# Weight gradient by Strassen pairs: sums carried by accumulating transfers, copies over two banks, and a twenty-fourth pair

## The chip, the core and the metric

The kernel runs on one core of a Trainium2 chip. The metric is the device time of one execution in microseconds, as the median of several runs. A profile of one execution goes with it; its span counts from the first to the last instruction on the core and is a little shorter than the metric (161.5 us against 163.29 us for the same run).

## The reference

```python
def setup_inputs():
    batch, m, k, n = 16, 512, 1024, 768
    input       : (batch, m, k) float32, random normal
    grad_output : (batch, m, n) float32, random normal

def reference(input, grad_output):
    return np.einsum('bmk,bmn->kn', input, grad_output).astype(np.float32)
```

So 8192 rows (16 x 512) of `input` and `grad_output` are contracted: out = X^T G, 1024 x 768. The rows are cut into 64 slabs of 128, and the result into four quarters: A and B are the upper 512 rows (k), C and D the lower ones; A and C take one half of the 768 columns (384), B and D the other. Each quarter has four banks' worth of result: q = 0 to 3, each 128 x 384.

## The kernel before

**Loads.** The slabs come in by twos. A unit u is two slabs (256 rows), and the transfers issued by GpSimd round float32 to bfloat16 on the way. `LOADS` says what a unit is: `s`, two slabs taken singly, or `P`, a pair.

```python
LOADS = "sssssssPPPPPPPPPPPPPPPPPPPPPPPss"      # 9 s, 23 P
PAIRS_HELD = 14                                  # buffers for units
...
for u, kind in enumerate(LOADS):
    ...
    if u >= MERGED:
        nc.gpsimd.dma_start(out=gp, in_=G[rows, :].rearrange("(p m) n -> p m n", m=2))
        nc.gpsimd.dma_start(out=xp, in_=X[rows, :].rearrange("(p m) k -> p m k", m=2))
    ...
    # an s unit becomes two items, a P unit one item
```

**Products.** A single slab costs 16 matmuls of 128 x 384: four quarters by four banks. A pair of slabs is handled as a 2 x 2 block product with seven products instead of eight (Strassen): `m n o p q`, kept in `macc`, and two that go straight to quarters A and D. That is 28 matmuls in place of 32, for five sums of operands on VectorE.

```python
def sum_g1(i): ... nc.vector.tensor_add(ge (128x1152), g[0:3*NH], g[NH:4*NH])
def sum_g2(i): ... nc.vector.tensor_sub(g[0::3], g[0::3], g[2:0:-1])
def sum_x1(i): ... nc.vector.tensor_add(xe[0:2], xp[0], xp[1])
def sum_x2(i): ... nc.vector.tensor_add(xe[2], ...)
def sum_x3(i): ... nc.vector.tensor_sub(x[1:3], x[1:3], x[0::3])
```

At the end the five products are shared out: A gets m + p - q, B gets o + q, C gets n + p, D gets m + o - n. In the kernel before VectorE does this with the operations named in `SHARES`, except that -q goes to A as the first contents of A's banks (the step `A38:0-q`).

```python
SHARE_OF = {
    "t1": ("m", "o", 0), "t2": ("p", "q", 0), "t3": ("q", None, 0),     # to A and B
    "l1": ("n", "m", Q), "l2": ("p", "o", Q), "l3": (None, "n", Q),     # to C and D
}
SHARES = ("l20 l21 l22 t20 t21 t22 t10 t11 t12 t13 l23 t23 l10 l11 l12 l13 l30 l31 l32 l33 ").split()
...
op(out=dst, in0=dst, in1=src)     # 128 x 768 where both sides are served, else 128 x 384
```

**Steps.** PSUM has eight banks, two groups of four. `ORDER` lists the steps: which sum (A to D, m to q) takes its items up to which number next, how many of its four banks ScalarE handles (after `:`), whether the sum is closed, that is emptied to SBUF, at the end of the step (`!`), and how many operations of the filler (operand sums, then shares) VectorE does ahead of each bank. A bank that ScalarE handles is first filled with the sum so far (`carry`), and the matmuls add to it; a bank that VectorE handles is added to the sum after the matmuls.

```python
ORDER = (
    "A1:3!0,0,0,0 C1:1 B1:3 B2!0,0,0,0 C2!0,0,0,0 D2:3 A2 D3 A3 D4!0,0,0,0 A4 B4:1^!0,0,0,0 C4 "
    "C6!0,0,0,0 A6!0,0,0,0 D6:2~!0,0,0,0 B6:3^ C8!0,0,0,0 ... "
    # ... cut ...
    "q23!3,0,0,0 m21:4~ m23!2,1,0,0 n21:4~ A38:0-q n23!5,0,0,1 A40 B18:4!2,1,0,1 A41!0,0,0,0 "
    "C17:3 C18!1,0,0,0 D41!3,0,0,0 "
).split()

def carry(m, slot, q):                                     # before the matmuls
    if q >= Q - byact:
        bank = psum.tile([P, 512], f32, name=f"bank{slot * Q + q}")[:, 0:NH]
        nc.scalar.copy(out=bank, in_=sum_of(p, q))         # L296
...
def mm(q, j):
    nc.tensor.matmul(bank, stat, mov, ...)                 # L337
...
def shut(q):                                               # after them
    fill(ahead[q])
    if act:        nc.scalar.copy(out=dst, in_=bank)               # L353
    elif fresh[p]: nc.vector.tensor_copy(out=dst, in_=bank)        # L355
    else:          nc.vector.tensor_add(out=dst, in0=bank, in1=dst)  # L357
    if final and p in "ABCD":
        nc.sync.dma_start(out=OUT[...], in_=dst)           # L360, the quarter's rows leave
```

The last bank of the last step is made in two pieces (L392, added at L400), so that its store starts sooner. At the start, twelve matmuls on constants (L96) warm TensorE, and the first two slabs are loaded as float32 and rounded by VectorE and ScalarE (L211).

```python
round_by("DVE", x0, xf[0], 0, P)            # columns of the first slab, in this order
round_by("ACT", x0, xf[0], 2 * P, 4 * P)
round_by("DVE", x0, xf[0], P, 2 * P)
round_by("DVE", x0, xf[0], 4 * P, 6 * P)
round_by("ACT", x0, xf[0], 6 * P, 8 * P)
...
if n == 1: round_by("DVE", g0, gf, 0, NH)   # right half of the first slab's gradient
```

Of the kernel before, what the change touches and what calls it, by code (L numbers as in the profile page):

```python
# [8 lines left out]

P = 128  # L10

LOADS = "sssssssPPPPPPPPPPPPPPPPPPPPPPPss"

ORDER = (
    "A1:3!0,0,0,0 C1:1 B1:3 B2!0,0,0,0 C2!0,0,0,0 D2:3 A2 D3 A3 D4!0,0,0,0 A4 B4:1^!0,0,0,0 C4 "
    "C6!0,0,0,0 A6!0,0,0,0 D6:2~!0,0,0,0 B6:3^ C8!0,0,0,0 B8!0,0,0,0 D8:2~!0,0,0,0 A8!0,0,0,0 "  # L20
    "D9:2 B10!0,0,0,0 D10!0,0,0,0 A10 B12:2^!0,0,0,0 A12!0,0,0,0 D12:3 B14!0,0,0,0 D14!0,0,0,0 "
    "C13:3^ C14!6,0,0,0 A15:1 1o2:4!1,1,1,0 q2:4!0,1,0,1 A16!0,0,0,0 D16:1^ p3:4!2,1,1,0 "
    "D17!0,0,0,0 n3:2 1o4:3!2,0,0,1 n4!0,0,0,0 m4:4!1,1,1,2 p5:1^!0,0,0,0 A19:3^!0,0,0,1 q4:4~ "
    "2q6!2,0,1,0 D20!1,0,0,0 o7:4~!0,1,1,1 n7:2^!1,0,0,1 m7:1^!1,0,0,0 p8:1~ 2A22:4!2,1,0,2 "
    "p9!0,0,0,0 D23:3~!0,0,1,0 q9:3^ 2q10!2,0,0,0 o10:2^!1,0,0,0 n10:2^ 2n11!2,0,0,0 "
    "A25:4~!1,0,1,0 m10:2^ 2m12!2,0,0,0 D26!1,0,0,0 p13:4~!0,1,2,1 o13:3~!0,0,1,1 q12:3~ "
    "2A28:2~!2,0,0,1 q13!0,0,0,0 n15:3~!2,0,1,1 D28:1^!0,0,1,0 o16:2^!0,0,0,0 q16:2~!2,0,0,1 "
    "m15:3~ 1p17:3^!4,0,1,1 D30!1,0,0,0 m16 m18!0,0,0,0 q18:4~!1,1,0,1 A32 1n19:4^!4,0,1,2 "
    "o20:1~!0,1,0,0 D34:3^ 4D35!1,0,0,0 A35!1,0,0,0 o22:2^ p21:4 5p23!1,0,1,1 o23!0,0,0,0 q21:2~ "
    "q23!3,0,0,0 m21:4~ m23!2,1,0,0 n21:4~ A38:0-q n23!5,0,0,1 A40 B18:4!2,1,0,1 A41!0,0,0,0 "  # L30
    "C17:3 C18!1,0,0,0 D41!3,0,0,0 "
).split()


SHARES = (
    "l20 l21 l22 t20 t21 t22 t10 t11 t12 t13 l23 t23 l10 l11 l12 l13 l30 l31 l32 l33 "
).split()

WARMUP = [512] * 10 + [128] * 2
PAIRS_HELD = 14  # L40
# [6 lines left out]
def kernel(  # L47
# [6 lines left out]
    nc = tc.nc  # L54
    bf16 = mybir.dt.bfloat16
    f32 = mybir.dt.float32

    B, M, K = input.shape
    _, _, N = grad_output.shape
    S = B * M // P  # L60
    KH = K // 2
    NH = N // 2
    Q = KH // P


    LEFT, RIGHT = slice(NH, N), slice(0, NH)
# [24 lines left out]
    nc.scalar.dma_start(out=xf[1], in_=X[P : 2 * P, :])  # L91

    ones = nc.const_aps.tensor(1.0, (P, P), bf16)
    wps = psum.tile([P, 512], f32, name="bank7")
    for cols in WARMUP:
        nc.tensor.matmul(  # L96
            wps[:, 0:cols],
# [105 lines left out]
    def fill(n):  # L203
        for _ in range(n):
            f, i = filler.pop()
            f(i)
# [36 lines left out]
            "A": lambda: (x[:, 1, k], ge[:, 2, :]),  # L243
        }[p]()

    def sum_of(p, q):
        if p in SLOT:
            return macc[:, SLOT[p], q, :]
        row = q if p in "AB" else Q + q
        return acc[:, row, 0:NH] if p in "AC" else acc[:, row, NH:N]  # L250

    done = {p: 0 for p in streams}
    fresh = {p: True for p in streams}
# [4 lines left out]

    def parsed(step):
        step, _, ahead = step.partition("!")  # L260
        step, _, byact = step.partition(":")
        early = byact[-1:] if byact[-1:] in ("^", "~") else ""
        byact = byact.rstrip("^~")
        at = next(c for c in step if c.isalpha())
        before, upto = step.split(at)
        ahead = [int(a) for a in ahead.split(",")] if ahead else None
        return int(before or 0), at, int(upto), int(byact[:1] or 0), byact[1:], early, ahead

    steps = [parsed(step) for step in ORDER]

# [1 line left out]
    def follower(n, free):  # L272
        now = {p for p in opened if p != steps[n][1]}
        shut_since = {steps[n][1]}
        for m in range(n + 1, len(steps)):
            _, p, _, byact, first, early, ahead = steps[m]
            if p not in now:
                if not free:
                    if not early:
                        return None  # L280
                    assert byact and not first and not fresh[p] and p not in shut_since
                    return m
                free -= 1
            now.add(p)
            if ahead is not None:
                now.remove(p)
                shut_since.add(p)
        return None
# [1 line left out]
    filled = {}  # L290

    def carry(m, slot, q):
        p, byact = steps[m][1], steps[m][3]
        if q >= Q - byact:
            bank = psum.tile([P, 512], f32, name=f"bank{slot * Q + q}")[:, 0:NH]
            nc.scalar.copy(out=bank, in_=sum_of(p, q))  # L296
            filled[m, q] = bank

    def visit(n):
        _, p, upto, byact, first, early, ahead = steps[n]  # L300
        close, last = ahead is not None, n == len(steps) - 1
        items_now = streams[p][done[p] : upto]
        done[p] = upto
# [1 line left out]
        if opening:  # L305
            slot = slots.pop(0)
            banks = []
            for q in range(Q):
                name = f"bank{slot * Q + q}"
                act = q >= Q - byact  # L310
                carried = act and not fresh[p]
                if carried:
                    assert name in used
                    if not early:
                        carry(n, slot, q)
                    bank = filled.pop((n, q))
                else:
                    bank = psum.tile([P, 512], f32, name=name)[:, 0:NH]
                if first:
                    assert name in used and not fresh[p] and not byact  # L320
                    src = macc[:, SLOT[first[1]], q, :]
                    if first[0] == "-":
                        nc.scalar.mul(out=bank, in_=src, mul=-1.0)
                    else:
                        nc.scalar.copy(out=bank, in_=src)
                used.add(name)
                banks.append((bank, carried or bool(first), act))
            if first:
                taken.add((p, first[1]))
            opened[p] = (slot, banks)  # L330
# [3 lines left out]
        def mm(q, j):  # L334
# [8 lines left out]
                skip_group_check=carried,  # L343
            )

        follows = follower(n, len(slots)) if close and not last else None

        def shut(q):
            fill(ahead[q])
            bank, _, act = banks[q]  # L350
            dst = sum_of(p, q)
            if act:
                nc.scalar.copy(out=dst, in_=bank)  # L353
            elif fresh[p]:
                nc.vector.tensor_copy(out=dst, in_=bank)  # L355
            else:
                nc.vector.tensor_add(out=dst, in0=bank, in1=dst)  # L357
            if final and p in "ABCD":
                row = q if p in "AB" else Q + q
                nc.sync.dma_start(out=OUT[:, row, LEFT if p in "AC" else RIGHT], in_=dst)  # L360
            if follows is not None:
                for b in ([q] if steps[follows][5] == "^" else range(Q) if q == Q - 1 else []):
                    carry(follows, slot, b)

        if len(items_now) == 1:
            for q in range(Q):
                mm(q, 0)
            if close:
                for q in range(Q):
                    shut(q)  # L370
        else:
            for q in range(Q):
                if last and q == Q - 1 and opening:
                    assert not banks[q][1]
                    break
                for j in range(len(items_now)):
                    mm(q, j)
                if close:
                    shut(q)
            else:  # L380
                q = None
            if q is not None:

                fill(ahead[q])
                dst = sum_of(p, q)
                row = q if p in "AB" else Q + q
                b0 = (LEFT if p in "AC" else RIGHT).start
                for c0, c1, name in ((0, 256, None), (256, NH, f"bank{slots[0] * Q}")):
                    bank = banks[q][0] if name is None else psum.tile([P, 512], f32, name=name)
                    for j in range(len(items_now)):  # L390
                        stat, mov = operands(p, items_now[j], q)
                        nc.tensor.matmul(  # L392
                            bank[:, 0 : c1 - c0],
                            stat,
                            mov[:, c0:c1],
                            start=j == 0,
                            stop=j == len(items_now) - 1,
                        )
                    d = dst[:, c0:c1]
                    nc.vector.tensor_add(out=d, in0=bank[:, 0 : c1 - c0], in1=d)  # L400
                    store = nc.sync if name is None else nc.scalar
                    store.dma_start(out=OUT[:, row, b0 + c0 : b0 + c1], in_=d)
        if close:
            fresh[p] = False
            del opened[p]
            slots.append(slot)

    rounded = False
    for n, (before, p, upto, *_) in enumerate(steps):
# [42 lines left out]
```

## Time and profile before

| what | value |
|---|---|
| time, median of 3 runs | 163.32 us (163.26 to 163.52) |
| span of the profiled execution | 161.5 us |
| TensorE (PE) busy | 157.4 us, 97%, 950 matmuls |
| VectorE (DVE) busy | 140.9 us, 87% |
| ScalarE (ACT) busy | 118.0 us, 73% |
| GpSimd (POOL) busy | 34.8 us, 22%, nearly all of it issuing loads |
| transfers on GpSimd's queue | 28.64 MB, 89.6% of the sixteen DMA engines over the span |
| granted TensorE clock | full throughout |

A matmul's bar in the trace is some 326 ns long, but the next one starts before it ends, so bars overlap; what counts is the step from start to start, which the chain of waits gives. Busy times of the other engines can be compared with the span directly. The DMA share is near full until about 141 us, when the last load has landed, and low after that, except for the stores at the end.

### The profile page before, as it was taken

What the parts mean: (1) busy time and instruction counts of PE and PEld (TensorE: products, weight loads), DVE (VectorE), ACT (ScalarE), POOL (GpSimd) and SP (SyncE); (2) the same over time, 40 slices, a digit from 0 to 9 for tenths busy, and PEclk for the clock granted to TensorE, in tenths of its full rate; (3) what the DMA queues carried; (4) which work ended last, traced back from release to release, by engine and by line L of the source; (5) the groups of instructions that cost most, each with busy time, mean ns of one, the idle gap of its engine ahead of it and who ended that gap; (6) DMA issues with size and microseconds to landing.
All of it is one profiled execution on the core that took longest, in us unless ns stands there. A gap on an engine that the chain in (4) does not pass through costs nothing.

```text
span 161.5 us, 2781 instructions
## 1 busy us (share of the span) xinstructions
PE 157.4 (97%) x950; PEld 92.8 (57%) x950; DVE 140.9 (87%) x267; ACT 118.0 (73%) x278; POOL 34.8 (22%) x69
## 2 busy tenths in 40 slices
PE   8999999999999999999999999999999999999991
PEld 2465655566555565655666665566665656656661
DVE  0545888979889999999999999999998999999982
ACT  3745358446598899978999897997795666987730
POOL 7442222122222212222212222222122100000000
PEclk9999999999999999999999999999999999999999
DMA  5999999999999999999999999999999999900695
GB/s 168 300 213 213 212 214 213 213 215 212 214 212 212 212 211 215 214 214 211 211 214 218 214 213 211 214 212 215 213 211 216 210 214 212 199 11 0 232 354 195
DMA packets 12398, 33.40 MB, mean 207 GB/s; under 512 B 1376, under 2 KB 4192, under 8 KB 12384
## 3 DMA queue, kind: packets, MB, share of 16 engines
q0 software_dynamic: 9360, 28.64, 89.6%
q1 hardware_dynamic: 2592, 3.47, 6.1%
q10 hardware_dynamic: 432, 1.11, 1.9%
q8 instruction: 7, 0.11, 0.3%
q14 instruction: 7, 0.06, 0.1%
HBM read 58.72 MB, written 3.15 MB: 383 GB/s over the span
## 4 chain that ended last, share of the span: by engine, by line
PE 84%; DMA 12%; issue 1%; DVE 0%; POOLq 0%
PE bank L337 84%; DMA xp<-in_input_dram 9%; DMA gp<-in_grad_output_dram 4%; PE bank L392 0%; DVE acc L400 0%; POOLq L436 0%
## 5 line engine op out<-in xcount | busy, mean ns | idle before, releaser
L337 PEld LDWEIGHTS <-xp 128*128 128x128 bf16 x650 | 63.3, 98 | 43.5 <-issue 0.8
L337 PE MATMUL bank<-gp,xp 128*128 128x384 bf16 x468 | 81.1, 327 | 0.1
L353 ACT COPY macc<-bank 128x384 f32<-128x384 f32 x91 | 39.4, 493 | 9.7 <-PE bank L337 9.4
L357 DVE TENSOR_TENSOR acc<-bank,acc 128x384 f32<-128x384 f32 x80 | 39.8, 552 | 5.8 <-PE bank L337 5.5
L337 PEld LDWEIGHTS <-xe 128*128 128x128 bf16 x276 | 26.9, 98 | 17.9 <-DVE xe L148 0.2
L353 ACT COPY acc<-bank 128x384 f32<-128x384 f32 x57 | 24.8, 485 | 13.9 <-PE bank L337 13.9
L296 ACT COPY bank<-macc 128x384 f32<-128x384 f32 x73 | 33.0, 496 | 1.6 <-DVE acc L357 0.9
L337 PE MATMUL bank<-ge,xp 128*128 128x384 bf16 x182 | 33.6, 326 | 0.0
L337 PE MATMUL bank<-gp,xe 128*128 128x384 bf16 x184 | 32.4, 326 | 0.0
L296 ACT COPY bank<-acc 128x384 f32<-128x384 f32 x47 | 21.6, 494 | 8.9 <-DVE acc L357 7.2
L114 POOL DMA_DIRECT2D xp<-in_input_dram x30 | 16.0, 532 | 53.0 <-DMA xp<-in_input_dram 30.2
L113 POOL DMA_DIRECT2D gp<-in_grad_output_dram x30 | 16.0, 533 | 37.3 <-PE bank L337 15.0
L357 DVE TENSOR_TENSOR macc<-bank,macc 128x384 f32<-128x384 f32 x35 | 18.1, 553 | 1.3 <-PE bank L337 1.3
L138 DVE TENSOR_TENSOR ge<-gp 128x1152 bf16<-128x1152 bf16 x23 | 17.3, 753 | 0.3 <-DMA gp<-in_grad_output_dram 0.3
L148 DVE TENSOR_TENSOR xe<-xp 128x1024 bf16<-128x1024 bf16 x23 | 15.8, 686 | 1.4 <-DMA xp<-in_input_dram 1.3
L194 DVE TENSOR_TENSOR acc<-acc,macc 128x768 f32<-128x768 f32 (+1 forms) x20 | 16.1, 875 | 0.0
L337 PE MATMUL bank<-ge,xe 128*128 128x384 bf16 x92 | 15.9, 326 | 0.0
L157 DVE TENSOR_TENSOR xp<-xp 128x1024 bf16<-128x1024 bf16 x23 | 15.8, 687 | 0.0
L143 DVE TENSOR_TENSOR gp<-gp 128x768 bf16<-128x768 bf16 x23 | 12.8, 555 | 0.5
L152 DVE TENSOR_TENSOR xe<-xp 128x512 bf16<-128x512 bf16 x23 | 9.7, 420 | 0.0
L355 DVE COPY acc<-bank 128x384 f32<-128x384 f32 x6 | 3.2, 555 | 3.3 <-PE bank L337 3.2
L96 PE MATMUL bank<-const-bfloat16-1.0 128*128 128x512 bf16 (+1 forms) x12 | 4.6, 574 | 0.8 <-PEq L436 0.8
(18 smaller groups left out, 15.7 us busy)
## 6 DMA issues: line engine op xcount, KB each, us to landing
xp<-in_input_dram POOLq DMA_DIRECT2D x30, 512.0 KB, 16.7
gp<-in_grad_output_dram POOLq DMA_DIRECT2D x30, 384.0 KB, 16.7
out_dram<-acc SPq DMA_DIRECT2D x15, 192.0 KB, 2.4
xf<-in_input_dram ACTq DMA_DIRECT2D x2, 512.0 KB, 5.0
gp<-in_grad_output_dram POOLq DMA_DIRECT2D x3, 192.0 KB, 6.5
xp<-in_input_dram POOLq DMA_DIRECT2D x2, 256.0 KB, 7.8
gf<-in_grad_output_dram SPq DMA_DIRECT2D x2, 192.0 KB, 4.3
out_dram<-acc SPq DMA_DIRECT2D x1, 128.0 KB, 1.9
```

Of the source, the lines that this page charges most:

```text
L113: nc.gpsimd.dma_start(out=gp, in_=G[rows, :].rearrange("(p m) n -> p m n", m=2))
L114: nc.gpsimd.dma_start(out=xp, in_=X[rows, :].rearrange("(p m) k -> p m k", m=2))
L138: nc.vector.tensor_add(out=ge.rearrange("p a n -> p (a n)"), in0=g[:, 0 : 3 * NH], in1=g[:, NH : 4 * NH])
L143: nc.vector.tensor_sub(out=g[:, 0::3, :], in0=g[:, 0::3, :], in1=g[:, 2:0:-1, :])
L148: nc.vector.tensor_add(out=xe[:, 0:2, :].rearrange("p a k -> p (a k)"), in0=xp[:, 0, :], in1=xp[:, 1, :])
L152: nc.vector.tensor_add(out=extra[i][0][:, 2, :], in0=xp[:, 0, 0:KH], in1=xp[:, 1, KH:K])
L157: nc.vector.tensor_sub(out=x[:, 1:3, :], in0=x[:, 1:3, :], in1=x[:, 0::3, :])
L194: op(out=dst, in0=dst, in1=src)
L296: nc.scalar.copy(out=bank, in_=sum_of(p, q))
L337: nc.tensor.matmul(bank, stat, mov, start=opening and j == 0 and not carried, stop=close and j == len(items_now) - 1, skip_group_check=car ...
L353: nc.scalar.copy(out=dst, in_=bank)
L357: nc.vector.tensor_add(out=dst, in0=bank, in1=dst)
```

## The change

The change has three named parts, and a new list of steps that goes with them.

- **A twenty-fourth pair.** The seventh unit of `LOADS` becomes a pair; eight `s` units and 24 `P` units remain.
- **Copies over two banks.** PSUM becomes one tile `ps` of eight banks, and a step may say (`@` and four bits) that two neighbouring banks are emptied, or filled, by one instruction of 128 x 2 x 384 instead of two.
- **Accumulating transfers.** When the last part of m, p or o has reached `macc`, a transfer issued by GpSimd adds the complete product to a quarter: m to D, p to C, o to D, each 128 x 4 x 384 float32. Product n goes to C as the first contents of C's banks (`C16:0+n`). VectorE keeps t1, t2, t3 and l3, and l1 and l2 are gone.

Their purpose is fewer matmuls, fewer instructions on ScalarE and VectorE, and fewer shares for VectorE near the end.

```diff
-LOADS = "sssssssPPPPPPPPPPPPPPPPPPPPPPPss"
+LOADS = "ssssssPPPPPPPPPPPPPPPPPPPPPPPPss"
 ORDER = (
-    "A1:3!0,0,0,0 C1:1 B1:3 B2!0,0,0,0 C2!0,0,0,0 D2:3 A2 D3 A3 D4!0,0,0,0 A4 B4:1^!0,0,0,0 C4 "
-    "C6!0,0,0,0 A6!0,0,0,0 D6:2~!0,0,0,0 B6:3^ C8!0,0,0,0 B8!0,0,0,0 D8:2~!0,0,0,0 A8!0,0,0,0 "
-    ... cut ...
+    "C1:3@1!0,0,0,0 B1:3@9 A2:1@7!0,0,0,0 B2@f D3:1@7 B3@9!0,0,0,0 D4@2!0,0,0,0 A4:1^@4!0,0,0,0 "
+    "C4@2!0,0,0,0 B4:2^@9 B6@9!0,0,0,0 D6:2~@e!0,0,0,0 C6@4 D8:2@8!0,0,0,0 C8@5!0,0,0,0 B8:1^@2 "
+    "A8:1^@5 ... "
+    ... cut ...
+    "q23:4@8 4q24@d!0,2,0,0 p24@6!0,0,0,0 n24@f!0,2,0,0 m24:4@f!0,0,0,0 B14 o24:3^@3!3,1,0,1 "
+    "B16!3,0,0,0 A40@9!0,2,0,0 C16:0+n@6!0,0,0,0 D40@3!4,0,0,0 "
 ).split()
 SHARES = (
-    "l20 l21 l22 t20 t21 t22 t10 t11 t12 t13 l23 t23 l10 l11 l12 l13 l30 l31 l32 l33 "
+    "t20 t21 t22 t23 t30 t31 t10 t11 t12 t13 t32 t33 l30 l31 l32 l33 "
 ).split()
+ADDED = "mD pC oD".split()
...
+    ps = psum.tile([P, 2 * Q, 512], f32, name="ps")
...
 def carry(m, slot, q):
         if q >= Q - byact:
-            bank = psum.tile([P, 512], f32, name=f"bank{slot * Q + q}")[:, 0:NH]
-            nc.scalar.copy(out=bank, in_=sum_of(p, q))
+            both = wide[2 + q // 2] and (q - q % 2) >= Q - byact
+            if both and q % 2 == 0:
+                return
+            b = q - both
+            nc.scalar.copy(out=ps[:, slot * Q + b : slot * Q + q + 1, 0:NH], in_=sum_of(p, b, q + 1))
...
 def shut(q):
+            both = wide[q // 2] and act == banks[q ^ 1][2] and not pieces
+            if both and q % 2 == 0:
+                return
             fill(ahead[q])
-            bank, _, act = banks[q]
-            dst = sum_of(p, q)
+            b = q - both
+            bank = ps[:, slot * Q + b : slot * Q + q + 1, 0:NH]
+            dst = sum_of(p, b, q + 1)
...
+        if final and p in SLOT:
+            for quarter in (pair[1] for pair in ADDED if pair[0] == p):
+                ...
+                nc.gpsimd.dma_start(
+                    out=sum_of(quarter, 0, Q), in_=sum_of(p, 0, Q), accum_op=mybir.AluOpType.add
+                )
```

The order in which the first slab's columns are rounded is not changed.

## The prediction

> **What bounds the kernel now.** I read the chain of waits first, because with 97% on TensorE the question is what sets its start and what follows its end.
>
> ```profile
> 1.23 6.26 DMA gp<-in_grad_output_dram
> 7.50 0.28 issue
> 7.78 13.91 DMA xp<-in_input_dram
> 21.68 0.04 issue
> 21.73 135.51 PE bank L337 x830
> 157.25 0.67 PE bank L392 x6
> ...
> 157.94 0.63 DVE acc L400 x2
> ```
>
> The columns are start, length and what. From 21.73 us to the end the chain is TensorE and nothing else: 830 matmuls in 135.51 us, 163.3 ns from start to start. Before that it is a load. All 128x384 matmuls at L337 are 932 - 6 = 926, so 926 - 830 = 96 were done at 21.73 us. The list of steps agrees: ahead of C8, the first step that uses items 6 and 7 (the fourth unit, u=3), stand six slabs of 16 matmuls. So TensorE stood there for u=3's `xp`. The waits of the weight loads, which stand for TensorE's, and the trace in order of time say how long:
>
> ```profile
> PEld L337 <- issue: 0.8, 4, 0.2
> PEld L337 <- DMA xp<-in_input_dram: 0.7, 2, 0.5
> PEld L337 <- DVE xp L211: 0.3, 1, 0.3
> PEld L337 <- DVE xe L148: 0.2, 1, 0.2
> ```
>
> ```profile
> 16.21 5.03 PEld L337 LDWEIGHTS <-xp 128*128 128x128 bf16 x32 [0.19 <-DMA xp<-in_input_dram]
> ...
> 21.73 4.34 PEld L337 LDWEIGHTS <-xp 128*128 128x128 bf16 x28 [0.48 <-DMA xp<-in_input_dram]
> ```
>
> Two waits for data, 0.19 and 0.48 us; after the second, nothing stops TensorE for more than 0.2 us. Next, the other engines and the transfers by stage (TensorE, weight loads, VectorE, ScalarE, GpSimd busy; clock, DMA share, GB/s):
>
> ```profile
> 100.00:120.00 20.00, 20.00 (x125) 12.05 (x124) 19.86 (x40) 17.87 (x43) 5.07 (x10) 1.00 1.07 213
> ...
> 140.00:145.00 5.00, 5.00 (x32) 2.95 (x31) 5.00 (x7) 4.91 (x13) 0.00 (x0) 1.00 0.26 52
> 145.00:150.00 5.00, 5.00 (x33) 3.03 (x31) 5.00 (x7) 3.80 (x10) 0.00 (x0) 1.00 0.00 0
> 150.00:155.00 5.00, 5.00 (x33) 2.96 (x31) 4.88 (x10) 3.39 (x9) 0.00 (x0) 1.00 0.84 301
> ```
>
> VectorE and ScalarE are nearly full, yet TensorE never waits for them: time saved on them buys nothing by itself. Loads end near 141.3 us (0.26 of the stage from 140 us).
>
> **What the Trainium skill says.** "TensorE: Matmul & The Clock Gate" (Wait — 56ns, not 53.3ns?) gives N / 2.4 GHz + 2.5 ns for back-to-back matmuls, 162.5 ns for N = 384; the trace's 163.3 agrees, so only the count of matmuls and waits can move the stretch. "ScalarE: Activation LUTs" (What ACT_TABLE_LOAD costs) has 0.833 ns per element on top of a fixed cost; the trace's 485 to 496 ns for 384 elements fit, and I use it for the copy over two banks. "DMA: Bandwidth & Descriptors" (SWDGE vs HWDGE vs iDMA) says that accumulation is for GpSimd's queue alone and that this has one context: such a transfer stands behind all loads issued earlier. The loads' 16.7 us from issue to landing show how long that queue is. The page gives no rate for accumulation and no trace here has one.
>
> **The change, part by part.** The rows for the copies and sums (busy us, mean ns):
>
> ```profile
> L357 DVE TENSOR_TENSOR acc<-bank,acc 128x384 f32<-128x384 f32 x80 | 39.8, 552 | 5.8 <-PE bank L337 5.5
> ...
> L357 DVE TENSOR_TENSOR macc<-bank,macc 128x384 f32<-128x384 f32 x35 | 18.1, 553 | 1.3 <-PE bank L337 1.3
> ...
> L194 DVE TENSOR_TENSOR acc<-acc,macc 128x768 f32<-128x768 f32 x16 | 14.1, 955 | 0.0
> ```
>
> *Matmuls.* Singles 16 slabs x 16 = 256, pairs 24 x 28 = 672: 928 against 18 x 16 + 23 x 28 = 932. Four fewer: 4 x 163.3 ns = **-0.65 us**, on the path.
>
> *Start.* In the new list item 6 is first used by D8. Ahead of it stand 88 matmuls, not 96: six slabs less A's share of items 4 and 5, which now comes in A8, after D8. u=3's load has nothing changed ahead of it and should land at 21.7 us again. Can TensorE have done 88 by then? The new list opens with C, whose columns are rounded last, and then needs the gradient's right half, which VectorE rounds only after C's first copy. From the starts in the trace (VectorE's three roundings end near 5.4 us, the second slab is rounded from 7.1 us) I get some 11 matmuls done at 8.0 us where the kernel before had 14. 11 + 77 x 0.163 us more is 20.6 us. So yes; it then waits 1.1 us instead of 0.48. Eight matmuls more stand after the wait: 8 x 163.3 ns = **+1.3 us**. From there 834 run up to the last bank, for 830: net **+0.65 us**. Later units come every 4.3 us (next 25.9, 30.2, 34.5 us) and are first used 1 to 2.5 us after landing, at 163.3 ns a matmul counted from 21.7 us, so this is the one data wait that I expect to set the path.
>
> *ScalarE.* By the new list 87 + 65 copies of one bank and 24 + 23 of two, for 148 + 120 of one. Before, 118.8 us for 268, 0.443 each; after, 152 x 0.443 + 47 x (0.443 + 0.32) = 103 us. -16 us, beside TensorE.
>
> *VectorE.* Adds: 57.9 us for 115, 0.503 each; after 72 x 0.503 + 20 x (0.503 + 0.403, from 955 - 552 ns) = 54.3. First copies +1.8. One more pair of sums, (17.3 + 12.8 + 15.8 + 9.7 + 15.8) / 23 = +3.1. Shares: 16.1 before; now 8 wide (t1, t2) at 0.88 and 8 narrow (t3, l3) at 0.503, 11.1. Sum -3.6 + 1.8 + 3.1 - 5.0 = -3.7 us, beside TensorE.
>
> *Transfers.* Each is 128 x 4 x 384 x 4 B = 0.786 MB. By t(n) = 21.7 + (n - 88) x 0.1633 us: p is complete at matmul 796, 137.3 us; m at 820, 141.3; o at 844, 145.2. The last step's first bank is done at matmul 901, 154.5 us. The transfer of p stands behind the last loads, so it starts near 141.3; m's behind it; o's adds to the same bytes as m's and must wait for m's landing. With A us for each, o's lands near 141.3 + 3A + 1.9 (1.9 from the store of 128 KB, as the cost of one landing and a new issue). Then VectorE still has four l3 (2.0), three adds (1.5) and the two pieces (0.63): 4.1 us. Without waiting, VectorE would end at 158.57 + 0.65 = 159.2. **Delay = 3A - 11.9 us**, if positive. For A I take estimates from this trace: 0.786 MB at 301 GB/s (the stores' stage) is 2.6 us; at the loads' 213 GB/s 3.7; at half the stores' rate, since source and destination are both read, 5.2. The first two delay nothing, the last 3.7 us.
>
> **Sum.** 163.32 + 0.65 = 164.0, plus a tail of 0 to 4 us. Weighed, 164.3.
>
> **The rivals.** *One:* the start is as good as before and the four matmuls count in full, 162.7 us. For it: a list this elaborate was plainly fitted, and the other waits vanish. Against it: 88 against 96 is a count, and u=3's landing belongs to the queue. *Two:* the accumulations become the bound, 166 to 170 us. For it: three in a row on one queue, behind the loads, two on the same bytes, and the DMA engines read twice. Against it: the engines are idle from 141.3 to 150 us. *Three:* bank turnover. A two-bank copy frees its first bank later (by 0.32 to 0.4 us), and TensorE waits, 0.5 to 1.5 us in all: 164.5 to 165.5. For it: short steps of four matmuls, 0.65 us. Against it: ScalarE has 16 us more room. *Four:* the lighter engines pay by 2%; nothing supports it, since TensorE waited for neither.
>
> **Range and chances.** No tail, some 55%: 163.6 to 164.5. Bank waits or a tail up to 2.6 us, 20%. A above 4.8 us, over 2% slower, 22%. Rival one and better, little. So 163.3 to 168.0; faster by over 2% 0.01, within 0.77, slower 0.22.
>
> **What would show it.** Right: a wait of about 1 us for `xp` near 20.6 us; 834 matmuls of 163 ns from 21.7 us to the last bank; no accumulation landing after 155 us. Wrong start: u=3's data used later than matmul 88, or landing earlier. Wrong tail: VectorE's l3 released by a transfer after 155 us, and TensorE's end well ahead of VectorE's. Wrong bank argument: weight loads released by ScalarE or VectorE for over 0.5 us in all.

## The result, and the profile after

169.81 us (median of 4 runs, 168.74 to 170.16) against 163.34 us: a ratio of 1.0383, interval 1.0336 to 1.043. The prediction was 164.3 us, in a range of 163.3 to 168.0. The time went where 3A - 11.9 looked for it, into the accumulating transfers at the end, but their cost was larger than reckoned and the way to the first of them was another.

The chain of waits of the kernel after (start, length, what):

```profile
7.67 13.99 DMA xp<-in_input_dram
...
21.71 119.31 PE ps L350 x728
...
142.41 0.74 ACT macc L373
143.15 0.29 issue
143.44 7.84 DMA acc<-macc
...
151.89 8.78 DMA acc<-macc
...
160.69 0.62 DVE acc L199 x2
...
164.05 0.53 DVE acc L421 x2
```

In the kernel before, the chain stayed on TensorE up to VectorE's last pieces. Here it leaves TensorE at 141 us (TensorE itself works on to 159.2 us), passes over ScalarE's last copies of m, and two accumulating transfers take over, m's into D (143.44 us) and o's into D (151.89 us). They are followed by VectorE's l3 shares, last adds and pieces. The start is as it was: TensorE released at 21.7 us by the fourth unit's `xp`. The trace in order of time shows the wait there (in brackets):

```profile
21.70 14.25 PEld L350 LDWEIGHTS <-xp 128*128 128x128 bf16 x89 [1.38 <-DMA xp<-in_input_dram]
21.71 14.47 PE L350 MATMUL ps<-gp,xp 128*128 128x384 bf16 x88 [0.99 <-DMA xp<-in_input_dram]
```

0.48 us before, 0.99 to 1.38 us now. At the other end, the stages show TensorE still at work and VectorE waiting (busy: TensorE, weight loads, VectorE, ScalarE, GpSimd; clock, DMA share, GB/s):

```profile
154.00:155.00 1.00, 1.00 (x9) 0.61 (x7) 0.73 (x1) 0.00 (x0) 0.00 (x0) 1.00 1.02 184
155.00:156.00 1.00, 1.00 (x8) 0.61 (x7) 0.00 (x0) 0.00 (x0) 0.00 (x0) 1.00 1.10 237
...
159.00:160.00 1.00, 0.23 (x5) 0.05 (x1) 0.00 (x0) 0.00 (x0) 0.00 (x0) 1.00 1.14 255
160.00:161.00 1.00, 0.00 (x0) 0.00 (x0) 0.31 (x1) 0.00 (x0) 0.00 (x0) 1.00 1.03 353
```

The DMA engines, which in the kernel before moved nothing from 142 to 150 us and only stores after that, are now full from 142 us on (1.12 from 142 to 150 us), but for about a microsecond around o's issue. TensorE ends at 159.2 us; VectorE starts again at 160.7. The granted clock has no part in this: its mean over the span is 0.987, but it is 1.00 up to 162 us and lower only after TensorE's last matmul. The groups, for the copies over two banks and for VectorE's wait (busy, mean ns, then idle time before them):

```profile
L373 ACT COPY macc<-ps 128x768 f32<-128x768 f32 x17 | 13.6, 801 | 7.9 <-PE ps L350 7.7
...
L377 DVE TENSOR_TENSOR acc<-ps,acc 128x768 f32<-128x768 f32 x8 | 7.6, 952 | 3.9 <-PE ps L350 3.9
...
L199 DVE TENSOR_TENSOR acc<-acc,macc 128x384 f32<-128x384 f32 x8 | 4.1, 550 | 6.0 <-DMA acc<-macc 6.0
```

ScalarE is busy for 104.7 us (118.0 before) and VectorE for 137.3 (140.9): VectorE is relieved by what was reckoned, ScalarE by somewhat less. The issues of the three transfers on GpSimd, in order p, m, o:

```profile
139.31 1.32 POOL L433 DMA_DIRECT2D acc<-macc  x1 [13.24 <-DVE acc L199]
143.44 1.30 POOL L433 DMA_DIRECT2D acc<-macc  x1 [2.80 <-ACT macc L373]
151.89 1.27 POOL L433 DMA_DIRECT2D acc<-macc  x1 [7.16 <-DMA acc<-macc]
```

The third waits 7.16 us for the second's landing, as both write D. What the engines did meanwhile I counted from the DMA packets that the trace lists; each transfer is 512 rows of 1536 B:

| rows of | first row starts, us | last row starts, us | took, us | rows a us |
|---|---|---|---|---|
| p into C | 141.2 | 145.7 | 4.5 | 113 |
| m into D | 145.7 | 150.8 | 5.0 | 102 |
| o into D | 154.1 | 160.1 | 6.0 | 85 |

An accumulated row occupies a DMA engine for 148 ns on average, a stored row of the same size for 70. Between m's last row and o's first lie 3.35 us. p's first row came 1.9 us after p's issue, while rows of the last loads still ran (the last of them started at 141.7 us); m's first came 2.3 us after m's issue and right behind p's last, o's 2.2 us after o's issue.

### The profile page after: what moved, and what is told of

Read it like the earlier page. It is cut to its first block, busy times and chain, and to the rows that moved or that the text cites. A ratio compares the mean times of both kernels' runs of the same rounds, so it can differ in the third digit from the quotient of the medians.

```text
span 167.9 us, 2669 instructions
## 1 busy us (share of the span) xinstructions
PE 157.4 (94%) x949; PEld 92.7 (55%) x949; DVE 137.3 (82%) x248; ACT 104.7 (62%) x209; POOL 38.8 (23%) x72
## 4 chain that ended last, share of the span: by engine, by line
PE 71%; DMA 22%; issue 2%; DVE 1%; ACT 1%; DVEq 0%; POOLq 0%; ACTq 0%
PE ps L350 71%; DMA acc<-macc 10%; DMA xp<-in_input_dram 8%; DMA gp<-in_grad_output_dram 4%; ACT macc L373 1%; DVE acc L199 1%; DVEq L476 0%; DVE acc L377 0%; DVE acc L421 0%; ACT ps L308 0%; POOLq L433 0%; POOLq L476 0%; ACTq L373 0%; POOLq L465 0%
## 5 line engine op out<-in xcount | busy, mean ns | idle before, releaser
L350 PE MATMUL ps<-gp,xp 128*128 128x384 bf16 x444 | 78.0, 327 | 1.1 <-DMA xp<-in_input_dram 1.0
L373 ACT COPY macc<-ps 128x384 f32<-128x384 f32 (+1 forms) x65 | 33.9, 573 | 16.5 <-PE ps L350 16.2
L377 DVE TENSOR_TENSOR acc<-ps,acc 128x384 f32<-128x384 f32 (+1 forms) x54 | 30.6, 608 | 8.0 <-PE ps L350 7.6
L350 PE MATMUL ps<-ge,xp 128*128 128x384 bf16 x187 | 34.8, 326 | 0.0
L350 PE MATMUL ps<-gp,xe 128*128 128x384 bf16 x192 | 33.4, 326 | 0.0
L373 ACT COPY acc<-ps 128x384 f32<-128x384 f32 (+1 forms) x46 | 22.5, 534 | 15.6 <-PE ps L350 15.3
L308 ACT COPY ps<-macc 128x384 f32<-128x384 f32 (+1 forms) x54 | 28.6, 562 | 3.0 <-DVE acc L377 1.4
L377 DVE TENSOR_TENSOR macc<-ps,macc 128x384 f32<-128x384 f32 (+1 forms) x38 | 24.3, 675 | 3.4 <-PE ps L350 3.2
L308 ACT COPY ps<-acc 128x384 f32<-128x384 f32 (+1 forms) x34 | 19.1, 598 | 5.5 <-DVE acc L377 5.3
L350 PE MATMUL ps<-ge,xe 128*128 128x384 bf16 x96 | 17.1, 326 | 0.0
L199 DVE TENSOR_TENSOR acc<-acc,macc 128x768 f32<-128x768 f32 (+1 forms) x16 | 11.1, 749 | 6.0 <-DMA acc<-macc 6.0
L148 DVE TENSOR_TENSOR gp<-gp 128x768 bf16<-128x768 bf16 x24 | 13.3, 554 | 0.6
```

The costliest lines, as they stand in the source:

```text
L148: nc.vector.tensor_sub(out=g[:, 0::3, :], in0=g[:, 0::3, :], in1=g[:, 2:0:-1, :])
L308: nc.scalar.copy(out=ps[:, slot * Q + b : slot * Q + q + 1, 0:NH], in_=sum_of(p, b, q + 1))
L350: nc.tensor.matmul(bank, stat, mov, start=opening and j == 0 and not carried, stop=close and j == len(items_now) - 1, skip_group_check=car ...
```

## The experiments

**o's addition back on VectorE.** (Each diff is against the kernel after, unless it says otherwise.)

```diff
-ADDED = "mD pC oD".split()
+ADDED = "mD pC".split()
-    "... t32 t33 l30 l31 l32 l33 "                      # SHARES
+    "... t32 t33 l20 l21 l22 l23 l30 l31 l32 l33 "
-    "... D40@3!4,0,0,0 "                                # ORDER
+    "... D40@3!8,0,0,0 "
```

> Only o's addition to D goes back from a transfer to VectorE (four additions of 128x384); m to D and p to C stay transfers. Theory 1, the second accumulation on D's bytes sets the end: VectorE waits for m's landing (151.3 us) at most, its stop from 154.7 to 160.7 us disappears, and it runs eight shares, three sums and two pieces from 154.7 us, 8 x 0.49 + 1.5 + 0.6 = 6.0, to some 160.8 us instead of 164.6: about 166.0 us. Theory 2, VectorE's own backlog at the end sets it and the transfer only hides it: 2 us more work, 169.8 to 172 us.

Measured: 165.28 us, ratio 1.012 (1.0081 to 1.016). VectorE in order of time:

```profile
153.90 3.82 DVE L199 TENSOR_TENSOR acc<-acc,macc 128x384 f32<-128x384 f32 x8
157.65 1.47 DVE L377 TENSOR_TENSOR acc<-ps,acc 128x384 f32<-128x384 f32 x3
```

The stop is gone, although VectorE does 2 us more: theory 1. VectorE has no pause left here and ends at 159.65 us, TensorE at 158.5, so part of theory 2 is true of this version: its backlog is the next bound. (In this trace the fourth unit landed 1 us sooner than in that of the kernel after, as the last section tells; the stop is gone by far more than that.)

**Copying instead of adding.** The additions are left out.

```diff
-    out=sum_of(quarter, 0, Q), in_=sum_of(p, 0, Q), accum_op=mybir.AluOpType.add
+    out=sum_of(quarter, 0, Q), in_=sum_of(p, 0, Q)
```

> The three transfers copy the product over the quarter instead of adding to it (the additions are left out). Same queue, same bytes, same waits. Theory 1a, the accumulation as such is slow (147 ns a row of 1536 B on a DMA engine where a stored row takes 67): rows near 70 ns, each transfer's rows done in some 2.2 us instead of 4.3, o's landing near 153 us, no wait of VectorE, 164 to 165 us. Theory 3, it is the place in the queue, the issue and the landing of any such transfer: rows may be faster but o still lands after 158 us, over 167.5 us.

Measured: 164.58 us, ratio 1.0072 (1.0055 to 1.0088). The chain, and the issue of o's transfer:

```profile
21.92 136.03 PE ps L350 x831
157.95 1.50 PE ps L413 x18
...
159.48 0.29 DVE acc L421
```

```profile
148.40 0.75 POOL L433 DMA_DIRECT2D acc<-macc  x1 [3.99 <-DMA acc<-macc]
```

TensorE sets the end again. The queue, bytes and waits are the same, but a transfer now lands 4.4 us after its issue (7.8 when adding), o's at 152.8 us, GpSimd is done with an issue in 0.75 us (1.3 when adding), and the packets hold up to three rows, 191 ns a packet on average and 66 ns a row. So it is the accumulation that is slow, not the place in the queue; theory 3 falls. This run also gives the kernel's time without its tail, 164.6 us.

**Without C's stores.** The four transfers that store quarter C are left out.

```diff
-            if final and p in "ABCD":
+            if final and p in "ABD":
```

> Quarter C is not stored (its four transfers to memory are left out), so that o's accumulation has the DMA engines to itself. Theory 1b, C's stores slow it (85 rows a us where m's had 124): 512 rows in 4.1 us instead of 6.2, 2 us less, about 167.8 us. If the stores only fill gaps: 169.8 us.

Measured: 169.4 us, ratio 1.0357 (1.0316 to 1.0399), which overlaps the interval of the kernel after; the time tells nothing. The packets do: o's rows took 5.35 us instead of 6.0, and its landing came 8.08 us after the issue instead of 8.78. From the chain:

```profile
150.94 8.08 DMA acc<-macc
```

C's stores cost some 0.7 us, not 2. The expected 2 us rested on 124 rows a us for m; the count gives 102 in the kernel after, which would have made it 1 us. What the other quarters' stores cost was not tried.

**A's items 4 and 5 ahead of C6.**

```diff
-D6:2~@e!0,0,0,0 C6@4
+D6:2~@e!0,0,0,0 A6!0,0,0,0 C6@4
```

> A takes items 4 and 5 in a step of its own ahead of C6, so that 96 matmuls and not 88 stand before the first use of the fourth unit. TensorE's wait of about 1 us goes, its end comes 1.3 us sooner (near 157.9 us). Theory 1, the tail is the transfers': p's rows wait for the loads and m's for p's, all as before, so 169.8 us, less than 0.5 us of change. Theory 4, the start and TensorE still count: 168.5 us.

Measured: 169.03 us, ratio 1.0345 (1.033 to 1.0361). TensorE's wait for the fourth unit is gone, its longest wait for a load 0.2 us. The issues of the three transfers, and VectorE's last pieces:

```profile
138.35 1.32 POOL L433 DMA_DIRECT2D acc<-macc  x1 [12.04 <-DVE acc L199]
142.47 1.30 POOL L433 DMA_DIRECT2D acc<-macc  x1 [2.80 <-ACT macc L373]
151.08 1.27 POOL L433 DMA_DIRECT2D acc<-macc  x1 [7.32 <-DVE acc L377]
```

```profile
163.04 0.61 DVE L421 TENSOR_TENSOR acc<-ps,acc 128x256 f32<-128x256 f32 x2
```

The chain still ends with two transfers, of 8.00 and 8.66 us, so theory 1 is right about what makes the tail. It is not right that p's rows wait for the loads and all stays as before. TensorE was 1 us ahead, p's and m's issues came 0.96 and 0.97 us sooner than in the kernel after, and VectorE ended 0.93 us sooner (163.65 us for 164.58); the fourth unit landed at 21.7 us in both traces. p's first row came at 140.3 us, 1.3 us ahead of the last row of a load. The median is 0.8 us lower, between the two expected times. So the traces show that an earlier start brings the whole tail sooner; the times alone, with their intervals overlapping, do not.

**o as first contents of D's banks.** ScalarE puts o into three of D's banks, as n is put into C's; the fourth, which is made in two pieces, gets it by one share.

```diff
-ADDED = "mD pC oD".split()
+ADDED = "mD pC".split()
-    "... t32 t33 l30 l31 l32 l33 "                      # SHARES
+    "... t32 t33 l23 l30 l31 l32 l33 "
-    "... D40@3!4,0,0,0 "                                # ORDER
+    "... 1D40:0+o@3!4,0,0,0 "
-                if first:
+                if first and not (last and q == Q - 1):
 ... the same condition once more, where the banks are listed
```

> o goes to D as the first contents of three of D's banks, filled by ScalarE in the last step, and by one share of VectorE for the fourth; m to D and p to C stay accumulating transfers. So the second accumulation on D's bytes goes and VectorE gets one share of 128x384 more, not four. Theory 1 (the chain of the two accumulations on D): m lands near 151 us, before VectorE needs D, and TensorE sets the end again as it did with plain copies: 164.5 us. Theory 2 (VectorE's backlog): 165 us or more, as with o's addition on VectorE (165.3).

Measured: 164.39 us, ratio 1.0049 (1.0035 to 1.0063), with m and p still accumulated by transfers. The end of the chain:

```profile
21.85 136.03 PE ps L350 x831
157.88 1.50 PE ps L413 x18
```

TensorE sets the end, and the tail of 5.4 us is gone with one accumulation, the one that had to wait for another.

**Both edits.** o by bank, and A6 ahead of C6.

> o by bank, and A's items 4 and 5 ahead of C6. With the tail no longer set by transfers the start should count: theory 1, 0.6 to 1.3 us less than o by bank alone, 163.2 to 163.9 us. If the start's eight matmuls were no loss: no difference.

Measured: 163.19 us, ratio 0.9986 (0.9979 to 0.9993); a second time, 163.19 us and 0.9989 (0.9981 to 0.9996). The chain:

```profile
6.81 15.82 PE ps L350 x96
22.63 0.01 issue
22.64 17.71 PE ps L350 x108
40.35 0.01 issue
40.35 116.55 PE ps L350 x711
156.91 1.50 PE ps L413 x18
```

Against o by bank alone, the start counts 1.2 us in the medians. It does so where the fourth unit lands late, as the last section tells: four of the 22 executions of o by bank took only 163.2 to 163.4 us. The version is faster than both kernels, by a tenth of a per cent over the one before. It still has 4 + 96 = 100 matmuls done at 22.64 us, where the kernel before had them at 21.73 + 4 x 0.163 = 22.4.

> The kernel with both edits once more beside it, on the same chip: 163.2 us, 0.1 to 0.2% under the kernel before.

**The same with copies over one bank.** Both edits, and:

```diff
-        wide = [int(wide or "0", 16) >> b & 1 for b in range(4)]
+        wide = [0] * 4
```

> As the kernel with both edits, but every copy and addition over one bank (the bits after @ are read as zero). ScalarE gets some 16 us more work and VectorE some 2 us. If copies over two banks only relieve engines that TensorE never waited for: within 0.5 us of the kernel with both edits. If they matter, because VectorE's end of the kernel has no room or because banks come free later: over 1 us slower; if they hurt bank turnover: faster.

Measured: 166.47 us, ratio 1.019 (1.0175 to 1.0206), 3.3 us more than with two banks. From the waits, of the weight loads and of the matmuls:

```profile
PEld L350 <- issue: 4.1, 9, 2.1
...
PE ps L350 <- DVE gp L148: 1.9, 1, 1.9
...
PEld L350 <- DVE xp L162: 1.0, 2, 0.8
```

TensorE itself now stops, once for 2.1 us (at 107 us; the matmul's own line puts 1.9 us down to the sum in `gp`) and once for 0.8 us, both times for an operand sum of VectorE, and VectorE ends at 161.4 us, 0.4 after TensorE. The copies over two banks are not a relief beside TensorE: this list of steps needs them.

**No accumulating transfer at all.** A's items 4 and 5 come ahead of C6, as in the last versions, but p, m and o are added by VectorE.

```diff
-ADDED = "mD pC oD".split()
+ADDED = "".split()
-    "... t32 t33 l30 l31 l32 l33 "                      # SHARES
+    "... t32 t33 l20 l21 l22 l23 l10 l11 l12 l13 l30 l31 l32 l33 "
-    "... C16:0+n@6!0,0,0,0 D40@3!4,0,0,0 "              # ORDER
+    "... 4C16:0+n@6!0,0,0,0 D40@3!8,0,0,0 "
```

> A's items 4 and 5 first, and no accumulating transfer at all: VectorE adds p to C and o to D (four additions of 128x768) and m to D (four of 128x384) as shares. If the transfers' purpose holds (they take work from a VectorE that is full at the end): VectorE's end comes some 3 us later than with o's additions alone on it, 167 to 168 us. If VectorE has room: 163.5 to 165 us.

Measured: 168.16 us, ratio 1.0289 (1.0276 to 1.0303). VectorE at the end:

```profile
157.37 3.83 DVE L199 TENSOR_TENSOR acc<-acc,macc 128x384 f32<-128x384 f32 x8
161.12 1.48 DVE L377 TENSOR_TENSOR acc<-ps,acc 128x384 f32<-128x384 f32 x3
```

It ends at 163.1 us, 4.6 us after TensorE (158.5), and the time is 2.9 us longer than with o's addition alone on VectorE. So p's and m's transfers together serve their purpose, and o's was one too many.

**The first rounding earlier.** Both edits, and:

```diff
-        if n == 1:
+        if n == 0:
             round_by("DVE", g0, gf, 0, NH)
 # and of the second slab, columns 0 to 4P are rounded ahead of 4P to 8P
```

> As the kernel with both edits, and the start in the order in which the new steps use it: VectorE rounds the first gradient's right half before C's first copy instead of after it, and of the second slab the columns that A and B use come first. In the kernel with both edits TensorE, after C's four matmuls, sat 0.6 to 0.85 us until 6.81 us for that right half, and from there never stopped for 0.3 us. If the start now counts in full: the right half is ready near 5.7 us, A's first matmul with the second slab some 7.2 us, 2 to 3 matmuls more are done by then, 0.3 to 0.45 us less, 162.75 to 162.9 us. If the landing of the fourth unit (21.7 us) or of the second slab absorbs it: 163.2 us.

Measured: 163.22 us, ratio 0.9988 (0.9979 to 0.9996): no gain over both edits. The chain's start:

```profile
1.17 5.06 DMA gf<-in_grad_output_dram
6.24 0.02 issue
6.26 0.37 DVE gp L216
```

The right half had landed only at 6.24 us; VectorE's order was not what held it. My expectation of 5.7 us took the data to be there.

## Why the prediction was wrong

**The start: right, for the landing that was reckoned.** 88 matmuls ahead of the fourth unit, a wait of 1.0 to 1.4 us for 1.1 reckoned, and its landing at 21.7 us. Without the tail the kernel stands at 164.4 to 164.6 us, for 164.0 reckoned. One count was off: the last step has nine items, not six, so 831 matmuls run up to the last bank and nine in it; the sum of 840 is the same. They took 163.7 ns each (136.03 us for 831), for 163.3. My figure of 20.6 us for the 88th would put the 100th at 22.55 us with no wait between; the version with both edits, which has none, had it at 22.64.

**The engines: right in size, wrong in worth.** ScalarE and VectorE fell by 13.3 and 3.6 us (16 and 3.7 reckoned). "Time saved on them buys nothing by itself" was read from the kernel before. For the new list it does not hold: with copies over one bank, 3.3 us are lost.

**The tail: the mechanism right, the size wrong.** The step that failed is the term A, the cost of one accumulating transfer, with the hand-over of 1.9 us beside it. The middle estimate, A = 3.7 us, puts o's landing at 141.3 + 11.1 + 1.9 = 154.3 us; it came at 160.67. The rows of p, m and o took 4.5, 5.0 and 6.0 us: 0.8, 1.3 and 2.3 too few in my sum, 4.4 together. Hand-over and last landing took 3.35 + 0.5 = 3.9 us, 2.0 more than taken from a store. 4.4 + 2.0 is the 6.4 us that were missing. VectorE then needed 3.9 us (4.1 reckoned) and ended at 164.58, 5.4 after the 159.2 reckoned without a tail. 163.34 + 0.65 + 5.4 = 169.4 us, 0.4 short of the median.

The choice behind it was the loads' rate of 213 GB/s. The better analogue stood beside it as the third estimate, half of the stores' rate: 5.2 us, close to the mean of 4.5, 5.0 and 6.0. But with the short hand-over even that gave 3.7 us of tail.

The first of the three A's came out by luck. The sum let p start when the loads end and m behind p. p's first row did come at 141.2 us, for 141.3 reckoned, but it followed p's own issue by 1.9 us (1.9 to 2.2 us in all nine traces with accumulating transfers) and not the end of the loads; with A's items ahead of C6 it came at 140.3 us. m's rows did begin where p's ended, at 145.7 us, but m was issued only at 143.44 us, after ScalarE's last copy of it. o's first row came 2.1 to 2.2 us after o's issue in three traces, with no transfer ahead of it. By that, m could not have begun before some 145.5 us in the kernel after even without p (an estimate). So the way ran from TensorE over m's last copy, as the chain has it, and p's rows cost the end next to nothing. A version without p's transfer but with o's was not run.

**The rivals.** The second (accumulations as the bound, 166 to 170 us) was the right one, and I gave it 22%. Its counter-argument, idle DMA engines from 141.3 us, said that there is room for three transfers and not that the last of them may land in time. The first fell, since the start was later. Of the third nothing is seen: no wait of TensorE put down to ScalarE in the kernel after, and 163.7 ns a matmul. Weight loads did wait for VectorE for 1.1 us in all, over the 0.5 us named as a sign, but for operand sums and the first roundings, not for banks, and 0.4 us at most on one line. The fourth found nothing for it. What the twenty-fourth pair is worth by itself was not tried.

## What to carry to other kernels

A transfer that adds costs its rows at the rate measured for adding, its issue and its landing; two that add to the same bytes cost these one after the other, so give such a target one addition at most near the end, and let a bank's first contents bring the other. Before counting saved matmuls, count those that stand ahead of each landing: what the list moves behind a wait is paid at the end. And slack that an old list of steps leaves an engine says little about a new list.

## What was not expected of the hardware

An accumulated row of 1536 B held a DMA engine for 145 to 151 ns in the kernel after, a stored one for 67 to 70 and one that was copied within on-chip memory, three to a packet, for 66. From m's last row to o's first passed 3.35 us, of which 2.2 lay between the issue and the first row.

The fourth unit did not always land at the same time: at 21.7 to 21.9 us in nine of the twelve traces, those of both kernels among them, but at 20.7 to 20.8 us in those of o on VectorE, without C's stores and with copies over one bank, with nothing changed ahead of it. The 22 times of o by bank fall in two groups that fit this, four from 163.2 to 163.4 us and eighteen from 164.2 to 164.8.

The traces show what goes with it. A transfer reports its landing in sixteen parts. In all twelve traces fifteen parts of this one were in by 20.4 to 20.7 us, and the late landing is the sixteenth alone. Each trace also has, in this stretch, one packet of 16384 B on the queue that the page calls q8, instruction, and it takes 0.89 to 0.95 us. It starts at 19.6 to 19.9 us where the landing is late, and at 20.3 to 20.6 us, when this load is nearly in, where it is early. That the packet holds up one DMA engine, and with it the sixteenth part, fits all twelve, but no run tested it. Why the packet comes sooner or later stays open.
